# Value products behind the last projection in three loops, other banks in a fourth, and loads cut to a loop's rows, in a nested self-attention kernel

## The chip, the cores and the metric

The kernel runs on one core of a Trainium2 chip. The metric is device time in microseconds (us). Three runs of the kernel before took 325.38, 325.65 and 325.74 us, so the median is 325.65. One further execution was recorded by the hardware profiler: it took 326.82 us, of which 325.0 us are the recorded span. Every row of a trace that is quoted comes from that one execution.

Engine names in the rows: PE is TensorE (matmuls; PEld its weight loads), DVE is VectorE, ACT is ScalarE, POOL is GpSimd, SP is SyncE, which here only issues DMAs.

## The reference

32 sequences of up to 512 rows, 512 wide, 8 heads of 64. The lengths are drawn between 64 and 511, the same draw each time. Rows past a sequence's length stay zero.

```python
for b in range(batch):
    seq_len = lengths[b]
    x_b = x[b, :seq_len].copy()
    qkv = np.matmul(x_b, w_qkv)
    q, k, v = np.split(qkv, 3, axis=-1)
    ...
    scores = scale * np.matmul(q, k.transpose(0, 2, 1))
    scores_max = np.max(scores, axis=-1, keepdims=True)
    attn = np.exp(scores - scores_max)
    attn = attn / (np.sum(attn, axis=-1, keepdims=True) + 1e-08)
    out_b = np.matmul(attn, v).transpose(1, 0, 2).reshape(seq_len, dim)
    output[b, :seq_len] = out_b
```

## The kernel before

**Loops.** The sequences are sorted by length on the chip, longest first, and taken in 16 pairs, 0 to 15. There is one loop for each count of rows N in 512, 448, 384, 352, 320 and so on down to 96, and a pair runs in the smallest N that holds its longer sequence. In this draw pair 0 runs in 512, 1 in 448, 2 in 384, 3 to 5 in 352, 6 in 320, 7 in 288, 8 in 256, 9 and 10 in 224, 11 in 192, 12 and 13 in 160, 14 in 128 and 15 in 96. A sequence is held in tiles of 128 rows; a loop has one to four of them.

**Positions.** The body of a loop has two positions, one for each sequence of the pair. A position does the attention of its own sequence, and between these steps the projections of the next sequence, whose transposed `x` (`xT`) must have landed. Five sequences ahead, SP loads `x` (LD). GpSimd casts it to 16 bit under a mask (C, line 374), and SP issues the transposing DMAs (XT, line 331) that make `xT` for the position after next. XT waits for the position's last projection on TensorE, since that is the last reader of the buffer it writes, and for C.

**Order.** The order in a position is written out by hand, one string for each N in the table `ORDER`. A step is a letter, a number, and after `@` the PSUM banks (0 to 7) that it writes:

- `S`: scores (line 1280), then their exponentials on ScalarE (line 1298).
- `Q`, `K`, `V`: projections (lines 303 and 314); `B` (queries and keys together), `U`, `V0a`, `V0b` (values) the same in half rows, in parts a, b, c (line 1334); `W` the values of the shared last tile (line 1221). The results are cast out of the bank by ScalarE (a, or `*`) or by VectorE (d).
- `A`: value products (line 1528, in halves line 1642). Loops whose last tile holds 64 rows or fewer pack the last tiles of both sequences into one; `Z` (line 1568) adds that shared tile's part to the products of two `A` steps. Behind a completed `A`, or behind `Z` for both of its `A` steps, VectorE normalises: U (lines 1743, 1704), R (lines 1739, 1695) and O (line 1677, which writes `out_nat`). Only then may another step use the bank.
- `X`: issue XT. `D`: issue LD. `L`, `P`: masks on VectorE and C. `E`: some columns. At the end of a position SP issues the store ST (line 1125), which waits for the last O.

Each engine runs its steps in this order, in its own queue. A wait is put where a step needs what another engine makes, or a bank that another engine still reads; it is a semaphore compared with a count kept in a register. These registers are raised once a pair, at the loop's end. For TensorE `LATE` says how many of its last steps come behind the raising (lines 2155 and 2158).

**Loads.** `load` (line 1106) brings whole tiles, with one DMA. In the last pairs of a count of tiles, the shorter form with one tile less is taken. Semaphores are raised by 16 for a landed DMA.

The step that the argument comes back to most is `rest` (the `Z` step), in its core:

```python
def rest(h0):
    pavs = [sums[h0][1], sums[h0 + 2][1]]
    ...
    op(f"z{h0}", "PE", matmuls, tuple(reads), held)
    for h in (h0, h0 + 2):
        normed(h)
```

Of the kernel before, what the change touches and what calls it, by code (L numbers as in the profile page):

```python
# [18 lines left out]
P = 128  # L19
# [18 lines left out]
    passed: object = None  # L38


LATE = {288: 3, 224: 3, 192: 1, 160: 3}


def plan_waits(head, bodies, entries, rare):
# [136 lines left out]
def kernel(  # L181
# [8 lines left out]
    nc = tc.nc  # L190
    B, MAXS, D = x.shape
    NT = MAXS // P
# [14 lines left out]
    def ring(n, shape, dtype, name, pool=const):  # L207
        return [pool.tile(shape, dtype, name=f"{name}{k}") for k in range(n)]
# [5 lines left out]
    x_bufs = ring(2, [P, NT, D], FP32, "x_nat")  # L214
# [20 lines left out]
    xv = x.rearrange("b (t p) d -> b p t d", p=P)  # L235
# [46 lines left out]
    }  # L282
# [9 lines left out]
    def tiles(N):  # L292
        return -(-N // P)
# [28 lines left out]

    def unit(name):

        return 16 * NT if name[:2] == "XT" else 16 if name[:2] in ("LD", "ST", "ZT") else 1

    def transpose(name, xT, x16, n, rows=P, pairs_on=0):

# [56 lines left out]
    def before_loops():  # L385
# [4 lines left out]
        def op(name, eng, emit, reads=(), writes=(), dma=False):  # L390
            ops.append(Op(name, eng, emit, tuple(reads), tuple(writes), dma))
# [16 lines left out]
        sp, act, dve, pool = nc.sync, nc.scalar, nc.vector, nc.gpsimd  # L408
# [44 lines left out]
        def warm(name, source, count, repeats, after):  # L453
# [4 lines left out]
            def matmuls():  # L458
# [11 lines left out]
                out=t,  # L470
                in_=blank,
# [34 lines left out]
        def key(lens, ids):  # L506
# [20 lines left out]
                out=t, in0=key_row, scalar1=key_col, scalar2=None, op0=ALU.is_lt  # L527
# [60 lines left out]
        for n in range(NT, 0, -1):  # L588
            N = min(N for N in LOOPS if tiles(N) == n)
# [37 lines left out]
        found = {}  # L627
# [11 lines left out]
            op(name, "SP", load, ("order",))  # L639

        def fetch(name, b, at, k, t0, t1):
            op(
                name,
                "SP",
                lambda: sp.dma_start(
                    out=x_bufs[b][:, t0:t1, :],
                    in_=xv[bass.ds(found[at][k], 1), :, t0:t1, :].rearrange("o p t d -> (o p) t d"),
                ),
                (),
                [f"xn{b}", *(f"xn{b}.{t}" for t in range(t0, t1))]  # L650
                if t1 - t0 == NT
                else [f"xn{b}.{t}" for t in range(t0, t1)],
                dma=True,
            )
# [9 lines left out]
        for t in range(NT):  # L664
            fetch(f"x0.{t}", 0, 0, 0, t, t + 1)
# [3 lines left out]
        weights("wk", w_k, D, NC // 2, NC)  # L669
        numbers("n1", 1, 4)  # L670
        fetch("x1.0", 1, 1, 0, 0, NT // 2)
        fetch("x1.2", 1, 1, 0, NT // 2, NT)

        warm("warm1", ones16, 12, 1, ())
# [6 lines left out]
                out=t,  # L681
# [27 lines left out]
                out=t, in_=shifted.rearrange("p (g k) -> p g k", k=4), axis=AX.X, op=ALU.add  # L709
# [120 lines left out]
        def joined(name, low, high, bits, after, out=None):  # L830

            t = const.tile([P, B // 2], FP32, name=f"h_{name}") if out is None else out
            op(
                name,
                "DVE",
                lambda: dve.scalar_tensor_tensor(
                    out=t, in0=high, scalar=float(2**bits), in1=low, op0=ALU.mult, op1=ALU.add
                ),
                after,
                (name if out is None else "table",),  # L840
            )
            return t

        def twos(source):
            return [source.rearrange("p (j two) -> p j two", two=2)[:, :, k] for k in range(2)]
# [4 lines left out]
        later = joined("later", *twos(order_i[:, 6 : B + 6]), 5, ("order",))  # L850
# [28 lines left out]
                out=alive[:, 0:B, :],  # L879
# [11 lines left out]
                out=queries[:, 1, :], in0=alive[:, 0, :], scalar1=2.0, scalar2=-1.0, op0=ALU.mult, op1=ALU.add  # L891
# [8 lines left out]
                out=t,  # L900
                in_=more[:, (448 - (NT - 1) * P) // 32 % 4 :: 4, :].rearrange("p k j -> p j k"),
# [11 lines left out]
                out=m_bufs[0], in0=alive[:, 2, :], scalar1=0.0, scalar2=None, op0=ALU.add  # L913
# [8 lines left out]
                out=v_bufs[0][:, :, :, HD],  # L922
# [8 lines left out]
        for half in range(2):  # L931
            for own in range(2):
                at_ = 1 - (half ^ own)
                k = B // 2 - at_
                rows = slice(half * P // 2, (half + 1) * P // 2)
# [6 lines left out]
                        out=to,  # L942
# [95 lines left out]
    def position(N, j, at, ring):  # L1038
# [4 lines left out]
        n = tiles(N)  # L1043
# [7 lines left out]
        o = 1 - j  # L1051
# [43 lines left out]
        def unless_past(ahead, name, transfer):  # L1095

            with nc.If_lt(own_pair, (B - ahead - j + 1) // 2):
                last = transfer()
                if last is not None:
                    last.then_inc(sems[name], 16)  # L1100
            with nc.Else():
                nc.sync.sem_inc(sems[name], unit(name))
            nc.end_ifs()

        def load(k=n):
            return nc.sync.dma_start(
                out=x_bufs[o][:, 0:k, :],
                in_=xv[bass.ds(here["later"][j], 1), :, 0:k, :].rearrange("o p t d -> (o p) t d"),
            )

        def load_live():
            name = f"LD{j}"
            with nc.sync.If_cmp(of(here["pairs"], "SP"), here["until"], "IS_LT"):
                load().then_inc(sems[name], 16)
            with nc.sync.Else():
                load(n - 1).then_inc(sems[name], 16)
            nc.sync.end_ifs()
# [650 lines left out]
        def maybe(name, ahead, transfer):  # L1768
            return transfer if n > 1 else lambda: unless_past(ahead, name, transfer)
# [6 lines left out]
        for step in steps(N, j):  # L1776
            step = step.split("@")[0]
            kind, act = step[0], step.endswith("*")
            if step[2:3] in ("a", "b", "c"):
                name, engines = step[:2], step[4:]  # L1780
# [66 lines left out]
            elif kind == "X":  # L1847
                transfer = maybe(f"XT{j}", 3, transposed)
# [60 lines left out]
    here = {}  # L1909
# [13 lines left out]
    for v in range(len(LOOPS)):  # L1923
        later = {op.name for body in bodies[v:] for op in body[0] + body[1]}
# [7 lines left out]
    rare = {"Y0", "Y1", "w", "W0", "W1"}  # L1932
# [32 lines left out]
    sems = {name: tc.alloc_semaphore(f"done_{name}") for name in lead}  # L1965
# [6 lines left out]
    def value_of(v, j, wait):  # L1972

        name = wait[1]
        if name in rare and wait[0] in ("iter", "iterin"):
            return wait[0].replace("iter", "rare"), lead[name] + 1 - wait[2]
        if wait[0] == "pos":
            return "pos", lead[name] + 1 - wait[2] + j
        if wait[0] == "iter":
            return f"iter{unit(name)}", unit(name) * (lead[name] + 1 - wait[2])  # L1980
        if wait[0] in ("posin", "posold"):
            return wait[0], lead[name] + 1 - wait[2]
        if wait[0] == "iterin":
            return f"iterin{unit(name)}", unit(name) * (lead[name] + 1 - wait[2])
        if wait[0] == "lead":
            return None, lead[name] * unit(name)
        if wait[0] == "last":
            last = max(u for u in range(len(LOOPS)) if name in has[u])
            return f"end{last}", lead[name]
        return None, 1  # L1990


    raised = {"pos": 2, "rare": 1, "iter16": 16, f"iter{16 * NT}": 16 * NT}
    entered = {"posold": 0, "posin": 2, "rarein": 1, "iterin16": 16, f"iterin{16 * NT}": 16 * NT}

    tails_of = []
    for v, N in enumerate(LOOPS):
        mine = [k for k, op in enumerate(bodies[v][1]) if op.eng == "PE"]
        tails_of.append(mine[len(mine) - LATE.get(N, 0) :])
        assert not any(bodies[v][1][k].skip for k in tails_of[v])  # L2000
# [99 lines left out]
    with tc.tile_critical():  # L2100
# [59 lines left out]
        for v, N in enumerate(LOOPS):  # L2160
# [17 lines left out]
            with nc.body(body):  # L2178
# [4 lines left out]
                p = nc.snap(pair, min_val=0, max_val=B // 2 - 1)  # L2183
# [59 lines left out]
```

## Time and profile before

| | before |
|---|---|
| median of three runs | 325.65 us |
| the profiled execution, its own time | 326.82 us |
| its span | 325.0 us |
| mean granted TensorE clock | 0.993 |
| LD issues of 768 KB / 512 KB / 1024 KB | 12 / 14 / 3 |
| XT issues (line 331) | 74, about 1.25 us of SP each |

A row of the timeline gives the start (us from the span's start), the length in us (of all the merged instructions), the engine, the line, the operation with what it writes and reads, the shape, the count, and in brackets the idle time before it with what ended it. A row of the chain gives start, length, engine and what ran. Line numbers are those of the kernel before. Matmuls are pipelined, so a row's length reaches past the start of the next one; what a matmul group takes is read from start to start.

### The profile page before, as it was taken

The page shows a single profiled execution, that of the slowest core. Times are in us where ns is not written, and L with a number is a line of the kernel's source. Part 1 is how long each engine was busy: PE and PEld are TensorE (multiplying, and loading weights), DVE is VectorE, ACT ScalarE, POOL GpSimd, SP SyncE. Part 2 cuts the span into 40 slices and gives each one's busy share as a digit, 9 for nine tenths or more (in the row PEclk, how much of TensorE's full clock was granted, in tenths as well). Part 3 has the DMA queues.
Part 4 walks back from the last instruction along what each step waited for, and adds up shares of the span by engine and source line. Part 5 has one row for each costly group of instructions (what it writes and reads, how often), then busy time and mean ns, then how long its engine had stood idle before and what let it go on. Part 6 is the DMA issues. An engine that isn't in the chain of part 4 may idle for free.

```text
span 325.0 us, 13310 instructions
## 1 busy us (share of the span) xinstructions
PE 311.3 (96%) x5092; PEld 202.2 (62%) x5092; DVE 193.4 (60%) x650; ACT 264.0 (81%) x415; POOL 100.6 (31%) x147
## 2 busy tenths in 40 slices
PE   7999999999999999999999999999999899999991
PEld 4444645555656556556556657657787787877861
DVE  6866566566665546456456456436575666666753
ACT  4489899797878988988988979898877678777761
POOL 2657040414030330330330342143222223533420
PEclk9999999999999999999999999999999999999997
DMA  6986858497848999597677777756459957896652
GB/s 216 373 316 72 259 180 277 94 351 171 281 50 281 224 294 261 185 285 226 227 225 226 244 210 198 221 169 219 135 150 206 233 179 178 180 239 161 216 180 81
DMA packets 69448, 68.85 MB, mean 212 GB/s; under 512 B 40720, under 2 KB 40720, under 8 KB 69392
## 3 DMA queue, kind: packets, MB, share of 16 engines
q1 hardware_dynamic: 69344, 68.12, 74.8%
q8 instruction: 33, 0.54, 0.7%
q14 instruction: 23, 0.19, 0.2%
q10 hardware_dynamic: 48, 0.00, 0.0%
HBM read 25.17 MB, written 33.55 MB: 181 GB/s over the span
## 4 chain that ended last, share of the span: by engine, by line
PE 88%; DMA 4%; DVE 2%; issue 1%; ACT 1%; SPq 1%; POOL 0%; POOLq 0%; DVEq 0%
PE banks L1334 43%; PE banks L1280 14%; PE banks L1528 12%; PE banks L314 7%; PE banks L303 6%; DMA xT<-x 3%; PE banks L1642 3%; PE banks L1221 1%; PE banks L1568 1%; DMA x_nat<-in_x_dram 1%; DVE out_nat L1677 0%; PE banks L768 0%; ACT et L1298 0%; SPq L331 0%; ACT xT L777 0%
## 5 line engine op out<-in xcount | busy, mean ns | idle before, releaser
L1298 ACT ACTIVATE et<-banks 128x704 f16<-128x704 f32 (+8 forms) x256 | 199.1, 825 | 25.8 <-PE banks L1280 22.0
L374 POOL TENSOR_TENSOR x<-x_nat,mask 128x512 f16<-128x512 f32 x82 | 83.1, 1039 | 177.1 <-DVE mask L1062 170.0
L1334 PE MATMUL banks<-xT,w_r 64*128 64x352 f16 (+9 forms) x1536 | 127.7, 294 | 1.4 <-DMA xT<-x 1.0
L1334 PEld LDWEIGHTS banks<-xT,w_r 64*128 64x128 f16 x1536 | 68.9, 94 | 37.8 <-PE banks L1334 8.7
L1280 PE MATMUL banks<-qz,kT 64*128 64x352 f16 (+11 forms) x624 | 77.4, 294 | 1.3 <-ACT et L1298 0.4
L1677 DVE SCALAR_TENSOR_TENSOR out_nat<-rcp,banks 128x256 f32<-128x256 f32 (+1 forms) x128 | 59.4, 470 | 6.5 <-DMA out_dram<-out_nat 2.2
L1378 DVE CAST qz<-banks 128x448 f16<-128x448 f32 (+6 forms) x47 | 26.4, 562 | 46.6 <-PE banks L1334 45.8
L1528 PEld LDWEIGHTS banks<-v_aug,et 128*128 128x128 f16 x1248 | 42.0, 97 | 14.4 <-issue 7.2
L1528 PE MATMUL banks<-v_aug,et 128*128 128x65 f16 x1248 | 47.6, 194 | 0.7 <-ACT et L1298 0.6
L1334 PE MATMUL banks<-w_r,xT 64*128 64x512 f16 (+1 forms) x368 | 46.6, 372 | 0.3 <-ACT v_aug L1500 0.3
L1280 PEld LDWEIGHTS banks<-qz,kT 64*128 64x128 f16 x624 | 28.0, 94 | 24.0 <-issue 5.9
L1743 DVE TENSOR_TENSOR rcp<-banks,queries 128x4 f32<-128x4 f32 (+1 forms) x110 | 17.3, 157 | 19.8 <-PE banks L1528 7.3
L1397 DVE CAST v_aug<-banks 128x512 f16<-128x512 f32 x25 | 16.6, 690 | 19.2 <-PE banks L1334 19.2
L314 PE MATMUL banks<-w_r,xT 128*128 128x512 f16 x104 | 26.7, 380 | 0.0
L1334 PEld LDWEIGHTS banks<-w_r,xT 64*128 64x128 f16 x368 | 17.1, 94 | 14.5 <-PE banks L1334 1.0
L303 PE MATMUL banks<-xT,w_r 128*128 128x160 f16 (+3 forms) x256 | 23.2, 243 | 1.1 <-issue 0.6
L1378 ACT CAST kT<-banks 128x352 f16<-128x352 f32 (+6 forms) x47 | 22.5, 479 | 1.5 <-PE banks L1334 1.5
L1739 DVE RECIPROCAL rcp<-rcp 128x4 f32<-128x4 f32 (+1 forms) x110 | 20.2, 184 | 3.8
L1378 DVE CAST kT<-banks 128x352 f16<-128x352 f32 (+5 forms) x33 | 17.9, 552 | 7.7 <-PE banks L1334 7.6
L303 PEld LDWEIGHTS banks<-xT,w_r 128*128 128x128 f16 x256 | 16.5, 98 | 6.2 <-issue 1.2
L1378 ACT CAST qz<-banks 128x352 f16<-128x352 f32 (+6 forms) x33 | 15.3, 464 | 3.4 <-PE banks L1334 3.3
L1500 ACT CAST v_aug<-banks 128x512 f16<-128x512 f32 x15 | 8.9, 590 | 9.5 <-PE banks L314 9.5
(117 smaller groups left out, 180.4 us busy)
## 6 DMA issues: line engine op xcount, KB each, us to landing
x_nat<-in_x_dram SPq DMA_DIRECT2D x12, 768.0 KB, 6.7
out_dram<-out_nat SPq DMA_DIRECT2D x12, 768.0 KB, 4.1
x_nat<-in_x_dram SPq DMA_DIRECT2D x14, 512.0 KB, 4.6
out_dram<-zeros SPq DMA_DIRECT2D x12, 512.0 KB, 3.7
out_dram<-out_nat SPq DMA_DIRECT2D x12, 512.0 KB, 5.1
out_dram<-out_nat SPq DMA_DIRECT2D x4, 1024.0 KB, 6.8
x_nat<-in_x_dram SPq DMA_DIRECT2D x3, 1024.0 KB, 7.0
out_dram<-zeros SPq DMA_DIRECT2D x4, 768.0 KB, 4.5
```

Of the source, the lines that this page charges most:

```text
L303: last = nc.tensor.matmul(dst[:, 0:N], w_r[:, c, w0 : w0 + P], xT[:, c, 0:N], start=(c == 0), stop=(c == NC - 1),)
L314: last = nc.tensor.matmul(pv, xT[:, c, t * P : (t + 1) * P], w_r[:, c, 2 * D : 3 * D], start=(c == 0), stop=(c == NC - 1),)
L374: return engine.tensor_tensor(out=x16, in0=x32, in1=live.broadcast_to([P, D]), op=ALU.mult)
L1280: last = nc.tensor.matmul(psc[par][:, x * wide : x * wide + N], kT[r, i, c0 : c0 + P], qz[r, i, 0:N], start=True, stop=True,)
L1298: return nc.scalar.activation(out=et[:, :, x0:x1, 0:N], in_=got.rearrange("p j (x q) -> p j x q", q=wide)[:, :, x0:x1, 0:N], func=AF.Exp, ...
L1334: last = nc.tensor.matmul(to, lhs(rows, c), rhs(rows, c), start=(c == 0 and opens), stop=(c == NC - 1 and not opens),)
L1378: return lambda copy, bank: copy(out=buf[:, ms, 0:M], in_=bank[:, 0 : gm * M].rearrange("p (m q) -> p m q", q=M),)
L1397: return lambda copy, bank: copy(out=v_bufs[o][:, t, :, 0:HD], in_=bank.rearrange("p (h d) -> p h d", d=HD))
L1528: last = nc.tensor.matmul(pav[:, g, qt, :], e_bufs[e][:, c0 + qt * P : c0 + (qt + 1) * P], v_aug[:, kt, h, :], start=(kt == 0 and not (hal ...
L1677: return nc.vector.scalar_tensor_tensor(out=o_t[:, 0:n, h0 * HD : (h0 + heads) * HD].rearrange("p t (g d) -> p t g d", d=HD), in0=by, scal ...
L1739: return nc.vector.reciprocal(out=r, in_=total if n == 1 else r)
L1743: return nc.vector.tensor_tensor(out=r.rearrange("p (t g) -> p t g", t=n), in0=total.rearrange("p (t g) -> p t g", t=n), in1=rows, op=ALU. ...
```

## The change

Three kinds of edit are made together.

**The order.** In 256 (second position) the last half B1b goes ahead of A0b, and A4 and A6 go behind the last projection and behind the issue of XT and LD. In 192 (second position) V0a and V0b go ahead of A1a and A1b by one step each, so that A1b ends up behind XT and LD. In 160, A2 and Z0 go behind the last projection and XT in both positions. In 288 (first position) S3 is put in banks 6 and 7 in place of 5 and 6. `LATE` gets an entry for 256.

```diff
-LATE = {288: 3, 224: 3, 192: 1, 160: 3}
+LATE = {288: 3, 256: 2, 224: 3, 192: 1, 160: 3}
...
-        288: "L P D S0@56 B2a@24 S5@01 B2b:aa S3@56 B0a@01 S1@23 S9@45 B0b:dd S2@67 B1a@32 S6@45 B1b:da S4@67 "
+        288: "L P D S0@56 B2a@24 S5@01 B2b:aa S3@67 B0a@01 S1@23 S9@45 B0b:dd S2@67 B1a@32 S6@45 B1b:da S4@67 "
...
-        "A1b | L P S0@01 U0a@25 S1@34 U0b:ad B0a@76 S2@01 E0@4 B0b A0a@23 B0c:da B1a@45 S3@01 A0b B1b A4@6 "
-        "A6@7 B1c:aa X D",
+        "A1b | L P S0@01 U0a@25 S1@34 U0b:ad B0a@76 S2@01 E0@4 B0b A0a@23 B0c:da B1a@45 S3@01 B1b A0b B1c:aa "
+        "X D A4@6 A6@7",
...
-        "P B0a@50 S1@34 B0b S2@67 B0c:da W0@4 S0@12 B1a@03 S3@67 E0@5 B1b A0a@12 B1c:aa A0b A1a@46 V0a@57 A1b "
-        "V0b:aa X D",
-        160: "L P S0@01 S1@23 V0@5 Q0*@4 A0@0 K0*@7 A2@1 S2@23 Z0 K2*@6 Q2*@7 X D A4@5 A6@2 Z4 | L P S0@34 S1@67 "
-        "K2@0 Q2*@1 A0@3 W0*@4 Q0@6 A2@5 K0*@0 Z0 S2@12 V0*@6 X D A4@4 A6@7 Z4",
+        "P B0a@50 S1@34 B0b S2@67 B0c:da W0@4 S0@12 B1a@03 S3@67 E0@5 B1b A0a@12 B1c:aa A0b V0a@57 A1a@46 "
+        "V0b:aa X D A1b",
+        160: "L P S0@01 S1@23 V0@5 Q0*@4 A0@0 K0*@7 S2@23 K2*@6 Q2*@7 X D A2@1 Z0 A4@5 A6@2 Z4 | L P S0@34 S1@67 "
+        "K2@0 Q2*@1 A0@3 W0*@4 Q0@6 K0*@0 S2@12 V0*@6 X D A2@5 Z0 A4@4 A6@7 Z4",
```

**The loads.** Where N is no multiple of 128, the last tile is loaded by a DMA of its own, and only to row N. The semaphore of a load then counts to 32, and a load of one DMA adds 16 by an instruction of SP.

```diff
-        return 16 * NT if name[:2] == "XT" else 16 if name[:2] in ("LD", "ST", "ZT") else 1
+        units = {"XT": 16 * NT, "LD": 32, "ST": 16, "ZT": 16}
+        return units.get(name[:2], 1)
...
         def load(k=n):
+            name, rows = f"LD{j}", N - (n - 1) * P
+            batch = bass.ds(here["later"][j], 1)
+            if k < n or rows == P:
+                nc.sync.sem_inc(sems[name], 16)
+                return nc.sync.dma_start(
...
+                )
+            partial = nc.sync.dma_start(
+                out=x_bufs[o][0:rows, n - 1, :],
+                in_=xv[batch, 0:rows, n - 1, :].rearrange("o p d -> (o p) d"),
+            )
...
+            partial.then_inc(sems[name], 16)
             return nc.sync.dma_start(
-                out=x_bufs[o][:, 0:k, :],
-                in_=xv[bass.ds(here["later"][j], 1), :, 0:k, :].rearrange("o p t d -> (o p) t d"),
+                out=x_bufs[o][:, 0 : n - 1, :],
+                in_=xv[batch, :, 0 : n - 1, :].rearrange("o p t d -> (o p) t d"),
             )
```

What stands in the engines' queues: first TensorE at the end of 256's second position and into the 224 loop, before and then after the change. The 1642 (1666) rows are halves of A0b, shown as their last two; the 1334 (1358) rows are projections; 1528 (1552) are A4 and A6; the branch ends the loop.

```order
827 L1642 MATMUL banks<-v_aug_68,et_82 128x65
828 L1334 MATMUL banks<-xT_75,w_r 128x224 x16
829 L1528 MATMUL banks<-v_aug_68,et_83 128x65 x8
830 L1528 MATMUL banks<-v_aug_68,et_84 128x65 x8
831 L1334 MATMUL banks<-xT_75,w_r 128x224 x8
832 L2086 UNCONDITIONAL_BRANCH
```

```order
827 L1666 MATMUL banks<-v_aug_68,et_81 128x65
828 L1666 MATMUL banks<-v_aug_68,et_82 128x65
829 L1358 MATMUL banks<-xT_75,w_r 128x224 x8
830 L2179 ISA
831 L2182 REGISTER_ALU
832 L1552 MATMUL banks<-v_aug_68,et_83 128x65 x8
833 L1552 MATMUL banks<-v_aug_68,et_84 128x65 x8
834 L2110 UNCONDITIONAL_BRANCH
```

The last eight projections now stand ahead of the sixteen products of A4 and A6, and the raising of the registers ahead of those.

Then TensorE in 160's second position, from Q0 on, before and after. The `128x160` rows of line 303 are Q0 and K0, 1568 (1592) are Z0 and Z4, 314 is V0, and 1280 (1304) is S2.

```order
1103 L303 MATMUL banks<-xT_75,w_r 128x160 x8
1104 L1528 MATMUL banks<-v_aug_68,et_82 128x65 x4
1105 L303 MATMUL banks<-xT_75,w_r 128x160 x8
1106 L1568 MATMUL banks<-v_aug_67,et_82 128x65 x8
1107 L1280 MATMUL banks<-qz_66,kT_70 128x160 x4
1108 L314 MATMUL banks<-w_r,xT_75 128x512 x4
1109 L2155 ISA
1110 L2158 ISA
1111 L1528 MATMUL banks<-v_aug_68,et_82 128x65 x8
1112 L1568 MATMUL banks<-v_aug_67,et_82 128x65 x8
```

```order
1103 L303 MATMUL banks<-xT_75,w_r 128x160 x16
1104 L1304 MATMUL banks<-qz_66,kT_70 128x160 x4
1105 L314 MATMUL banks<-w_r,xT_75 128x512 x4
1106 L1552 MATMUL banks<-v_aug_68,et_82 128x65 x4
1107 L1592 MATMUL banks<-v_aug_67,et_82 128x65 x8
1108 L2179 ISA
1109 L2182 ISA
1110 L1552 MATMUL banks<-v_aug_68,et_82 128x65 x8
1111 L1592 MATMUL banks<-v_aug_67,et_82 128x65 x8
```

A2 (four products) and Z0 (eight) went from between the projections to behind V0, the last of them. The queues of VectorE, ScalarE and GpSimd are the same as before.

More of the change, by code (lines that the diff above doesn't have):

```diff
@@ L641, in fetch, with transfer @@
         def fetch(name, b, at, k, t0, t1):
+            def transfer():
+                if name in sems:
+                    sp.sem_inc(sems[name], 16)
+                return sp.dma_start(
+                    out=x_bufs[b][:, t0:t1, :],
+                    in_=xv[bass.ds(found[at][k], 1), :, t0:t1, :].rearrange("o p t d -> (o p) t d"),
+                )
             op(
@@ L644, in fetch @@
                 "SP",
[L645 to L648, printed above, removed]
+                transfer,
                 (),
@@ L1105, in load @@
         def load(k=n):
+            name, rows = f"LD{j}", N - (n - 1) * P
[3 more added lines that the diff above has]
+                return nc.sync.dma_start(
+                    out=x_bufs[o][:, 0:k, :],
+                    in_=xv[batch, :, 0:k, :].rearrange("o p t d -> (o p) t d"),
+                )
+            partial = nc.sync.dma_start(
+                out=x_bufs[o][0:rows, n - 1, :],
+                in_=xv[batch, 0:rows, n - 1, :].rearrange("o p d -> (o p) d"),
+            )
+            if n == 1:
+                nc.sync.sem_inc(sems[name], 16)
+                return partial
+            partial.then_inc(sems[name], 16)
             return nc.sync.dma_start(
-                out=x_bufs[o][:, 0:k, :],
-                in_=xv[bass.ds(here["later"][j], 1), :, 0:k, :].rearrange("o p t d -> (o p) t d"),
+                out=x_bufs[o][:, 0 : n - 1, :],
+                in_=xv[batch, :, 0 : n - 1, :].rearrange("o p t d -> (o p) t d"),
             )
@@ L1990, in value_of @@
         return None, 1
-    raised = {"pos": 2, "rare": 1, "iter16": 16, f"iter{16 * NT}": 16 * NT}
-    entered = {"posold": 0, "posin": 2, "rarein": 1, "iterin16": 16, f"iterin{16 * NT}": 16 * NT}
+    raised = {"pos": 2, "rare": 1, "iter16": 16, "iter32": 32, f"iter{16 * NT}": 16 * NT}
+    entered = {"posold": 0, "posin": 2, "rarein": 1, "iterin16": 16, "iterin32": 32, f"iterin{16 * NT}": 16 * NT}
     tails_of = []
```

## The prediction

> **What bounds the kernel now.** I read the page first (busy shares, then the chain that ended last), then the waits, then the timelines at the five places where the order changes.
>
> ```profile
> PE 311.3 (96%) x5092; PEld 202.2 (62%) x5092; DVE 193.4 (60%) x650; ACT 264.0 (81%) x415; POOL 100.6 (31%) x147
> ...
> PE   7999999999999999999999999999999899999991
> ...
> PE 88%; DMA 4%; DVE 2%; issue 1%; ACT 1%; SPq 1%; POOL 0%; POOLq 0%; DVEq 0%
> ```
>
> TensorE is busy for 311.3 of 325.0 us and holds 88% of the chain. The change takes no matmul away, so it can only shorten what is left, 13.7 us. Of the 40 slices of 8.1 us the first is 0.7 busy and the last 0.1, so most of that is the start and the end. Of the transposing DMA (line 331), which the change issues earlier, the view of that line says who waits:
>
> ```profile
>   PE banks L1334: 1.0, 1
>   PE banks L303: 0.5, 1
> DMA to landing us min/median/max: 2.3/3.1/7.3
> ```
>
> TensorE waits for it twice, for 1.0 and 0.5 us. The other side of the ledger is VectorE: a value product that runs later is normalised later, and the bank that it filled comes free later. So each edit is weighed by two things: what an earlier transpose pays, and what a later normalisation costs.
>
> **256, second position (before the 224 loop).** Timeline of TensorE, then the chain, then SP:
>
> ```profile
> 243.89 0.66 PE L1528 MATMUL banks<-v_aug,et 128*128 128x65 f16 x16
> 244.48 1.05 PE L1334 MATMUL banks<-xT,w_r 64*128 64x224 f16 x16
> ...
> 250.74 1.13 PE L1642 MATMUL banks<-v_aug,et 64*128 64x65 f16 x64
> 252.82 0.56 PE L1334 MATMUL banks<-xT,w_r 64*128 64x224 f16 x8 [0.96 <-DMA xT<-x]
> ```
> ```profile
> 245.18 1.21 SPq L331
> 246.43 6.25 DMA xT<-x
> ```
> ```profile
> 241.56 0.42 SPq L1106 DMA_DIRECT2D x_nat<-in_x_dram  x1
> 242.23 0.38 SPq L1125 DMA_DIRECT2D out_dram<-out_nat  x1
> ```
>
> A4 and A6 (16 matmuls, 243.89 to 244.48, so 0.59 us) move behind the last projection, so SP may issue the transposes 0.59 sooner. The wait at 252.82 is 0.96, so all 0.59 could come out of it. But this transpose lands 6.25 us after its issue, against a median of 3.1, behind a load (241.56) and a store (242.23) of 512 KB each. What the queue still holds doesn't leave earlier because the transposes come earlier. The gain is therefore between 0 and 0.59; I take **-0.2**, the lower third, because the load and the store stand ahead either way.
>
> The Trainium skill, "DMA: Bandwidth & Descriptors", section "Two DMAs through the same engine are not ordered", says that within one queue of one DMA engine descriptors start in order. By that alone the term would be 0, and by an idle queue 0.59; the 6.25 us of this row side with the page.
>
> The same edit swaps A0b with B1b (16 projections, 0.77 in the chain). Its normalisation starts 0.77 later:
>
> ```profile
> 243.68 0.75 DVE L1677 SCALAR_TENSOR_TENSOR out_nat<-rcp,banks 128x256 f32<-128x256 f32 x2
> 247.74 0.62 DVE L1378 CAST qz<-banks 128x448 f16<-128x448 f32 x1 [0.43 <-PE banks L1334]
> ```
>
> It ends at 244.43 now and at 245.2 then, and the 224 loop's first projection (near 244.97, bank 3) needs that bank: up to 0.27 lost, and VectorE's cast at 247.74 slips by up to 0.7. Both lie ahead of the wait of 0.96, which absorbs them. If that cover is gone, they cost 0.3. The counters raised two operations ahead only move two register instructions off the loop's end: at most 0.1, counted at nothing.
>
> **288, other banks.** S3 goes to banks 6 and 7, so S9 no longer waits for S3's exponential:
>
> ```profile
> 212.99 0.30 PE L1280 MATMUL banks<-qz,kT 64*128 64x288 f16 x2 [0.36 <-ACT et L1298]
> ```
> ```profile
> 212.25 2.95 ACT L1298 ACTIVATE et<-banks 128x576 f16<-128x576 f32 x5
> 215.46 1.74 ACT L1298 ACTIVATE et<-banks 128x576 f16<-128x576 f32 x3
> ```
>
> The 0.36 goes, but ScalarE runs its exponentials back to back there (five in 2.95 us), so TensorE meets the next one instead. Between 0 and 0.36; I take **-0.05**.
>
> **192, second position.** V0b moves ahead of A1b:
>
> ```profile
> 284.20 0.31 PE L1642 MATMUL banks<-v_aug,et 64*128 64x65 f16 x8
> 284.46 0.61 PE L1334 MATMUL banks<-w_r,xT 64*128 64x256 f16 x8
> ...
> 290.06 0.37 PE L303 MATMUL banks<-xT,w_r 128*128 128x160 f16 x3 [0.65 <-issue]
> ```
>
> The projection, and the transpose that waits for it, come 0.26 sooner (284.46 less 284.20). No TensorE wait stands behind this transpose, and 0.65 us of waiting for nothing that the profile shows stands soon after, which can swallow it. Between 0 and 0.26; I take **-0.05**.
>
> **160, both positions: the largest term.** A2 and Z0 go behind the last projection. Z0 completes the shared last tile, and the whole normalisation chain (L1743, L1739, L1677, four times, 0.74 us each) starts only after it. TensorE of pairs 12 and 13 and of the 128 loop, then VectorE:
>
> ```profile
> 291.26 1.28 PE L303 MATMUL banks<-xT,w_r 128*128 128x160 f16 x16
> ...
> 294.70 0.30 PE L1568 MATMUL banks<-v_aug,et 64*128 64x65 f16 x8
> ...
> 295.07 1.04 PE L314 MATMUL banks<-w_r,xT 128*128 128x512 f16 x4
> 295.94 0.41 PE L1528 MATMUL banks<-v_aug,et 128*128 128x65 f16 x8
> ...
> 297.09 1.04 PE L314 MATMUL banks<-w_r,xT 128*128 128x512 f16 x4
> ...
> 309.54 1.03 PE L314 MATMUL banks<-w_r,xT 128*128 128x512 f16 x4
> ...
> 311.63 1.53 PE L303 MATMUL banks<-xT,w_r 128*128 128x96 f16 x32 [0.48 <-DMA xT<-x]
> ```
> ```profile
> 289.97 0.42 DVE L1677 SCALAR_TENSOR_TENSOR out_nat<-rcp,banks 128x256 f32<-128x256 f32 x1 [1.14 <-DMA out_dram<-out_nat]
> ...
> 295.04 0.16 DVE L1743 TENSOR_TENSOR rcp<-banks,queries 128x4 f32<-128x4 f32 x1 [0.42 <-PE banks L1568]
> ...
> 295.87 0.42 DVE L1677 SCALAR_TENSOR_TENSOR out_nat<-rcp,banks 128x256 f32<-128x256 f32 x1 [0.46 <-DMA out_dram<-out_nat]
> ...
> 296.61 0.42 DVE L1677 SCALAR_TENSOR_TENSOR out_nat<-rcp,banks 128x256 f32<-128x256 f32 x1
> ...
> 308.40 0.42 DVE L1677 SCALAR_TENSOR_TENSOR out_nat<-rcp,banks 128x256 f32<-128x256 f32 x1
> ```
>
> End of pair 12. Without A2 (0.12) and Z0 (0.13 to the next start) ahead of it, the projection at 295.07 starts at 294.82 and runs 0.87 (to the next start, 295.94); A2 starts at 295.69, Z0 at 295.81, and 0.34 later, as now, VectorE: 296.15 in place of 295.04. The first normalisation comes 0.41 behind that (295.87 less 295.04 less the wait of 0.46, rounded up), at 296.56; it no longer waits for the store, so of the 1.11 only 0.69 is late. The second starts at 297.30 and ends at 297.72. The next position's first projection (V0, bank 5) needs that second one. It starts at 297.09, just behind the 297.03 where it ends now: there is no slack. So **+0.7** (0.5 to 0.9, by how early TensorE really reaches Z0).
>
> Inside pair 12 Z0 goes from before the 16 projections (to 290.26) to behind them, so the normalisation at 289.97, now held 1.14 by a store, would start near 290.8, and the second end near 291.95; the second half of the projections at 291.26 (eight, from about 291.8) needs it: 0.1. VectorE's later key cast, which the projection just before Z0 waits for, gives another 0.1. Pair 13 is alike: together **+0.4** (0.1 to 0.6).
>
> Before the 128 loop the last normalisation ends at 308.82; moved like the first by 1.11 it ends at 309.9, and V0 at 309.54 waits for it: +0.4. In exchange the wait of 0.48 for the transpose at 311.63 goes, since its issue is 0.25 sooner and TensorE comes 0.4 later: **-0.1** (-0.48 to +0.3, the latter if the next transpose slips as well).
>
> **Loads.** Six in 352, four in 224 and two in 192 become two DMAs and bring 64 to 128 KB less.
>
> ```profile
> x_nat<-in_x_dram SPq DMA_DIRECT2D x12, 768.0 KB, 6.7
> x_nat<-in_x_dram SPq DMA_DIRECT2D x14, 512.0 KB, 4.6
> ```
> ```profile
> POOL x L374 <- DMA x_nat<-in_x_dram: 7.1, 2, 4.8
> ```
>
> The loads are issued five sequences ahead and land in 4.6 to 6.7 us; the only two waits for one, on GpSimd, are in the start, whose loads are not cut. What remains is SP's time, one issue more (0.4, as at 241.56) ahead of the next transposes, against some fewer bytes: bounds -0.2 and +0.4, taken as **0**.
>
> **The sum**: -0.2 - 0.05 - 0.05 + 0.7 + 0.4 - 0.1 + 0 = **+0.7**. The profiled execution took 326.82 us (span 325.0), so it would be 327.5 under a profile; the median of the runs is 325.65, so 326.35. 0.2% of this kernel is 0.65 us, about what a measurement can tell from no change: the forecast lies just above that bound.
>
> **Rivals.**
>
> *B, the transposes pay and the lag is covered: faster.* In full, the gains are 0.59 (256), 0.36 (288), 0.26 (192) and 0.48 (128 loop's wait), together 1.69. If Z0's lag finds cover (the normalisation, freed of the store's 0.46, is late by less than 0.3, which decides it), some 0.4 of stalls remain: -1.3, 324.35. For it: two real transpose waits. Against it: V0 at 297.09 has 0.06 of slack.
>
> *C, nothing to measure.* Half of the gain (0.8) meets half of the loss (0.6 to 0.8), or the wait of 0.65 at 290.06 shrinks by as much as the new ones cost: 325.65, give or take 0.3.
>
> *D, SP becomes late too: slower.*
>
> ```profile
> 287.99 1.18 SPq L1106 DMA_DIRECT2D x_nat<-in_x_dram  x1
> ...
> 291.58 3.97 SPq L331 DMA_TRANSPOSE xT<-x  x2
> ```
> ```profile
> DMA to landing us min/median/max: 2.3/3.5/4.7
> ```
>
> These transposes (291.58, and the second at 294.36, landed 2.3 later at 296.7) feed V0 at 297.09. The load at 287.99 held SP for 1.18; cut in two, it may hold it that long twice, and the transposes then land near 297.9, behind even the late normalisation (297.72). It decides from 1.1 us of delay. Here it costs 0.2 more than A, and the other ten cut loads at 0.05 to 0.1 each bring the sum to +1.4 to +1.9: 327.3. Against it: other loads are issued in 0.4.
>
> The Trainium skill, "SBUF — State Buffer", section "Summary: rules for kernel authors", speaks against cutting a transfer: "one DMA, not several". By the fit in that page's section "The DMA setup-cost knee", 2 us and the bytes over 436 GB/s, I estimate 3.2 us for 512 KB and 2.4 and 2.6 us for the two parts; the trace shows 4.6 for the whole, and nobody waiting for it.
>
> **Chances.** Forecast A 0.55 (from +0.1 to +1.2; 0.22 of it within 0.2%), B 0.2, C 0.15, D 0.1. So faster 0.2, same 0.22 + 0.15 = 0.37, slower 0.33 + 0.1 = 0.43. For 8 in 10 the range cuts half of B and most of D: 324.6 to 327.1.
>
> **What would show it.** Right: V0 at the start of pair 13 waits about 0.7 for `out_nat`, V0 of the 128 loop for the same, the wait of 0.48 there is gone, and the 0.96 before 252.82 is shorter by 0.2 (0.59 would be the gain in full, 0 the queue's). S9 in 288 has no wait, and a later score has one. Wrong: no wait for `out_nat` at pair 13, which gives B, or transposes issued later than now with the landing waited for, which gives D.

## The result

The changed kernel is slower: 328.61 us (median of 14 runs, 327.21 to 331.46) against 325.89 (14 runs of the kernel before). The ratio is 1.0076, with a 95% interval of 1.0054 to 1.0099, so +2.5 us (1.8 to 3.2; the two medians alone differ by 2.7). The direction was the one forecast; the size, +0.7, was far too small, and the time lies outside the range. The profiled execution took 328.77 us, its span 326.7.

The page of the changed kernel, for the rows shown of before:

```profile
PE 312.3 (96%) x5092; PEld 201.7 (62%) x5092; DVE 194.5 (60%) x650; ACT 263.7 (81%) x415; POOL 100.8 (31%) x147
...
PE   7999999999999999999999999999999999899982
...
PE 88%; DVE 5%; issue 2%; ACT 2%; DMA 1%; POOL 0%; SPq 0%; DVEq 0%; POOLq 0%
```

With the same matmuls TensorE is busy 1.0 us longer, and in the chain VectorE went from 2% to 5% while the DMAs went from 4% to 1%. In these two executions waits for the transpose went, and waits for VectorE came. (Lines moved: 1280 is now 1304, 1334 is 1358, 1528 is 1552, 1568 is 1592, 1677 is 1701, 1739 is 1763, 1500 is 1524; 303 and 314 stayed.)

**Where it came from.** The view by stretches, cut at three starts that both kernels have: the first scores of pair 12's second position, of pair 13, and of the 128 loop, up to the first projections for 96. The columns are the length and the busy time of TensorE, its weight loads, VectorE, ScalarE and GpSimd (counts in brackets), the granted clock, the DMA share and GB/s. Before:

```profile
290.74:296.49 5.75, 5.75 (x101) 4.71 (x98) 3.82 (x18) 4.32 (x8) 2.44 (x3) 1.00 0.76 185
296.49:307.42 10.93, 10.73 (x184) 8.73 (x178) 8.26 (x36) 8.80 (x15) 4.97 (x6) 1.00 0.64 196
307.42:311.63 4.21, 3.74 (x60) 2.93 (x61) 2.72 (x11) 2.60 (x5) 1.04 (x1) 1.00 0.84 255
```

After:

```profile
290.60:296.76 6.16, 6.15 (x100) 4.75 (x96) 3.96 (x18) 4.36 (x7) 2.45 (x4) 1.00 0.60 181
296.76:308.73 11.97, 11.51 (x184) 8.76 (x179) 7.74 (x34) 8.39 (x14) 4.97 (x6) 1.00 0.68 218
308.73:313.50 4.77, 3.91 (x64) 2.96 (x61) 3.79 (x16) 2.59 (x5) 1.04 (x1) 1.00 0.61 177
```

The same work takes 20.89 us before and 22.90 after: +0.41, +1.04 and +0.56, at a clock of 1.00 in both. Between these two executions the span grew by 1.7 us (325.0 to 326.7), so the 2.0 us of these stretches are more than all of it, and the rest of the span came out 0.3 shorter. Four kinds of row make them up. First, TensorE at the start of pair 13, as forecast:

```profile
295.80 0.28 PE L1552 MATMUL banks<-v_aug,et 128*128 128x65 f16 x4
296.01 0.30 PE L1592 MATMUL banks<-v_aug,et 64*128 64x65 f16 x8
296.24 0.42 PE L1552 MATMUL banks<-v_aug,et 128*128 128x65 f16 x8
296.60 0.30 PE L1592 MATMUL banks<-v_aug,et 64*128 64x65 f16 x8
296.76 0.86 PE L1304 MATMUL banks<-qz,kT 64*128 64x160 f16 x12
297.98 1.04 PE L314 MATMUL banks<-w_r,xT 128*128 128x512 f16 x4 [0.36 <-DVE out_nat L1701]
```

From the scores to V0 it was 0.60 (296.49 to 297.09) and is 1.22: V0 waits 0.36 idle, and the scores, whose second half needs the bank of the first normalisation, take 0.86, of which 0.3 are a wait for `out_nat`.

Second, in the same rows, a cost that the forecast did not have: A2's four products take 0.21 to the next start (295.80 to 296.01), where they took 0.12 in the forecast's reading, and Z0 takes 0.23, not 0.13. Z0 (64 rows) now stands between two groups of 128 rows; before, it stood next to S2, which also has 64.

Third, inside the pair, the projections behind the second position's scores:

```profile
291.11 1.47 PE L303 MATMUL banks<-xT,w_r 128*128 128x160 f16 x16
292.41 0.29 PE L1552 MATMUL banks<-v_aug,et 128*128 128x65 f16 x4
```

They take 1.30 to the next start, where they took 1.12 (291.26 to 292.38). About 0.2 of that is a wait for `out_nat`, between the first eight and the last eight.

Fourth, the 128 loop:

```profile
311.43 1.02 PE L314 MATMUL banks<-w_r,xT 128*128 128x512 f16 x4 [0.40 <-DVE out_nat L1701]
...
313.50 1.53 PE L303 MATMUL banks<-xT,w_r 128*128 128x96 f16 x32 [0.46 <-DVE v_aug L1524]
```

V0 waits 0.40 for the last normalisation, as forecast. But the wait of 0.48 for the transpose did not go: one of 0.46 for VectorE stands in its place. A wait of 0.20 for ScalarE ahead of that loop's first scores (307.42 before) is gone, since TensorE comes later.

Ahead of the 224 loop TensorE has two new waits, for the normalisation and for VectorE's cast, and the wait of 0.96 for the transpose is gone:

```profile
245.03 0.56 PE L1358 MATMUL banks<-xT,w_r 64*128 64x224 f16 x8 [0.32 <-DVE out_nat L1701]
...
248.96 1.04 PE L1358 MATMUL banks<-w_r,xT 64*128 64x512 f16 x8 [0.45 <-DVE qz L1402]
```

### The profile page after: what moved, and what is told of

Its sections match the earlier page's. It is cut to its first block, busy times and chain, and to the rows that moved or that the text cites. A ratio compares the mean times of both kernels' runs of the same rounds, so it can differ in the third digit from the quotient of the medians.

```text
span 326.7 us, 13366 instructions
## 1 busy us (share of the span) xinstructions
PE 312.3 (96%) x5092; PEld 201.7 (62%) x5092; DVE 194.5 (60%) x650; ACT 263.7 (81%) x415; POOL 100.8 (31%) x147
## 4 chain that ended last, share of the span: by engine, by line
PE 88%; DVE 5%; issue 2%; ACT 2%; DMA 1%; POOL 0%; SPq 0%; DVEq 0%; POOLq 0%
PE banks L1358 43%; PE banks L1304 13%; PE banks L1552 12%; PE banks L314 7%; PE banks L303 5%; PE banks L1666 3%; DVE out_nat L1701 2%; PE banks L1245 1%; PE banks L1592 1%; DMA x_nat<-in_x_dram 1%; DVE rcp L1763 1%; ACT et L1322 1%; PE banks L774 0%; DVE v_aug L1524 0%; ACT x L374 0%
```

## The experiments

Each kernel was timed in five rounds against the kernel before. A difference in us is worked out from the ratio, so it can be some tenths away from the difference of two medians. The theories: late normalisation in 160 carries the loss; or the cut loads do; or the other loops.

### The parts alone

The edit of 160 alone:

```diff
-        160: "L P S0@01 S1@23 V0@5 Q0*@4 A0@0 K0*@7 A2@1 S2@23 Z0 K2*@6 Q2*@7 X D A4@5 A6@2 Z4 | L P S0@34 S1@67 "
-        "K2@0 Q2*@1 A0@3 W0*@4 Q0@6 A2@5 K0*@0 Z0 S2@12 V0*@6 X D A4@4 A6@7 Z4",
+        160: "L P S0@01 S1@23 V0@5 Q0*@4 A0@0 K0*@7 S2@23 K2*@6 Q2*@7 X D A2@1 Z0 A4@5 A6@2 Z4 | L P S0@34 S1@67 "
+        "K2@0 Q2*@1 A0@3 W0*@4 Q0@6 K0*@0 S2@12 V0*@6 X D A2@5 Z0 A4@4 A6@7 Z4",
```

> The kernel before with the edit of 160 alone. If the late normalisation in 160 carries the loss: +1.5 to +2.5 us (0.7 at pair 13's start, 0.4 inside the pairs, 0.5 at the 128 loop, and some 0.2 per position for a 64-row matmul group that now stands alone between 128-row groups). If the loads or the other loops carry it: under +0.7. In the trace by the first theory: V0 of pair 13 waits 0.3 to 0.4 for out_nat, V0 of the 128 loop 0.4.

328.22 us (six runs) against 326.21, ratio 1.0057 (1.0038 to 1.0076): +1.9 us. Its three stretches take 6.17, 11.95 and 4.79, so 22.91 us, the same as the whole change to 0.01, with nearly the same waits (0.36, 0.43 and 0.46).

The loads alone (only the loads' hunks of the diff):

```diff
+            partial = nc.sync.dma_start(
+                out=x_bufs[o][0:rows, n - 1, :],
...
+            partial.then_inc(sems[name], 16)
```

> The kernel before with the cut loads alone. If the loads only cost SP's time, hidden: within 0.3 us of before. If they disturb the queue or the supply of instructions: +0.7 to +1.5, with more spread between runs, and longer waits for nothing shown (issue) on TensorE in 224 and 192.

328.02 us, ratio 1.0047 (1.0025 to 1.0069): +1.5 us. The cut loads, taken as free, are not. TensorE has one long new wait, ahead of 96's projections, and it is for the transpose:

```profile
307.15 5.26 DMA xT<-x
312.42 0.26 issue
312.68 1.53 PE banks L303 x32
```
```profile
312.68 1.53 PE L303 MATMUL banks<-xT,w_r 128*128 128x96 f16 x32 [1.53 <-DMA xT<-x]
```

The first rows are from the chain (start, length, what ran), the last from TensorE's timeline. Ahead of 307.15 the chain runs through SP, not TensorE.

256's order and its entry in `LATE` alone:

```diff
-        "A1b | L P S0@01 U0a@25 S1@34 U0b:ad B0a@76 S2@01 E0@4 B0b A0a@23 B0c:da B1a@45 S3@01 A0b B1b A4@6 "
-        "A6@7 B1c:aa X D",
+        "A1b | L P S0@01 U0a@25 S1@34 U0b:ad B0a@76 S2@01 E0@4 B0b A0a@23 B0c:da B1a@45 S3@01 B1b A0b B1c:aa "
+        "X D A4@6 A6@7",
```

> The kernel before with 256's order and its entry in LATE alone. If the earlier transpose pays its wait of 0.96 less the new waits of 0.32 and 0.45: -0.2 to -0.4. If the lead is given back at the next stall of instruction supply, as in the profile of after (0.54 at 254.4): 0 to +0.2.

326.40 us, ratio 1.0017 (1.0001 to 1.0033): not a gain, rather +0.5. Both new waits are there (0.32 and 0.45), and no wait for the transpose. No wait for nothing shown (issue) followed in this profile, so that reading was not borne out. The interval reaches almost to no change, and the size of this cost is uncertain.

288's banks and 192's order alone:

```diff
-        288: "L P D S0@56 B2a@24 S5@01 B2b:aa S3@56 B0a@01 S1@23 S9@45 B0b:dd S2@67 B1a@32 S6@45 B1b:da S4@67 "
+        288: "L P D S0@56 B2a@24 S5@01 B2b:aa S3@67 B0a@01 S1@23 S9@45 B0b:dd S2@67 B1a@32 S6@45 B1b:da S4@67 "
...
-        "P B0a@50 S1@34 B0b S2@67 B0c:da W0@4 S0@12 B1a@03 S3@67 E0@5 B1b A0a@12 B1c:aa A0b A1a@46 V0a@57 A1b "
-        "V0b:aa X D",
+        "P B0a@50 S1@34 B0b S2@67 B0c:da W0@4 S0@12 B1a@03 S3@67 E0@5 B1b A0a@12 B1c:aa A0b V0a@57 A1a@46 "
+        "V0b:aa X D A1b",
```

> The kernel before with the edits of 288 and 192 alone. By the profile of after 288 gains 0.2. 192 by the forecast: 0 to -0.26; if it costs, as the later start of 160 in the profile of after suggests (0.4 more of a stall at 283): +0.2 to +0.4. So -0.4 to +0.2 in all.

325.70 us against 326.21, ratio 1.0002 (0.9979 to 1.0024): nothing to measure. The trace has a possible reason why a small lead made in 288 does not show: TensorE comes to pair 12's second position early and waits there for the transpose.

```profile
289.69 1.27 PE L303 MATMUL banks<-xT,w_r 128*128 128x160 f16 x16 [0.37 <-DMA xT<-x]
```

### Parts taken out of the whole

> The change without its edit of 160 (so the loads, 256, 288 and 192 remain). If 160 and the loads each cost by themselves and cover one another in part: between +0.8 and +1.8 us, like the loads alone. If the loss of the loads was only scatter: within 0.5 of before.

Without 160's edit: 326.94 us, ratio 1.0024 (1.0006 to 1.0043), +0.8. The loads remain, and so does their wait: 1.33 for the transpose ahead of 96's projections. But this kernel holds the loads and 256's edit, which cost +1.5 and +0.5 alone; +2.0 is outside the interval here (0.2 to 1.4). So these two don't add either, or one of them is smaller than it looked; no run decides which.

> The whole change but for the loads. If 160's late normalisation covers what the cut loads cost at the end: 0.2 to 0.4 us less than the whole change, so +1.8 to +2.3 against before. If the two add: 1.5 less, +1.0.

Without the loads: 328.58 us, ratio 1.0081 (1.0054 to 1.0107), as slow as the whole change (1.0076). Its stretches take 22.91 us. So the loads cost 1.5 alone and nothing that can be measured on top of 160: where the normalisation in 160 is late, TensorE reaches 96's projections after the transpose has landed. In the profile of the whole change it landed at 312.4 (issued 307.97, 4.4 to landing), and the projections start at 313.50. Both are delays into one meeting point, and the later one counts.

### What in 160 costs

S2 and Z0 taken apart, nothing moved behind the last projection:

```diff
-        160: "L P S0@01 S1@23 V0@5 Q0*@4 A0@0 K0*@7 A2@1 S2@23 Z0 K2*@6 Q2*@7 X D A4@5 A6@2 Z4 | L P S0@34 S1@67 "
-        "K2@0 Q2*@1 A0@3 W0*@4 Q0@6 A2@5 K0*@0 Z0 S2@12 V0*@6 X D A4@4 A6@7 Z4",
+        160: "L P S0@01 S1@23 V0@5 Q0*@4 A0@0 K0*@7 S2@23 A2@1 Z0 K2*@6 Q2*@7 X D A4@5 A6@2 Z4 | L P S0@34 S1@67 "
+        "K2@0 Q2*@1 A0@3 W0*@4 Q0@6 A2@5 S2@12 K0*@0 Z0 V0*@6 X D A4@4 A6@7 Z4",
```

> The kernel before, with the 64-row groups S2 and Z0 of 160 no longer next to each other, each between 128-row groups, while Z0 stays ahead of the last projections and its end moves by at most 0.25 us. If a change between 64-row and 128-row matmuls costs TensorE about 0.09 us by itself: TensorE's starts in pairs 12 and 13 stretch by 0.19 per position, +0.5 to +0.9 in all. If only the late normalisation costs: 0 to +0.3.

326.96 us, ratio 1.0029 (1.0005 to 1.0052): +0.9 (0.2 to 1.7). TensorE in pair 13's first position, then the same groups before:

```profile
298.95 0.72 PE L303 MATMUL banks<-xT,w_r 128*128 128x160 f16 x8
299.60 0.31 PE L1280 MATMUL banks<-qz,kT 64*128 64x160 f16 x4
299.84 0.30 PE L1528 MATMUL banks<-v_aug,et 128*128 128x65 f16 x4
300.07 0.30 PE L1568 MATMUL banks<-v_aug,et 64*128 64x65 f16 x8
300.30 1.28 PE L303 MATMUL banks<-xT,w_r 128*128 128x160 f16 x16
```
```profile
298.64 0.72 PE L303 MATMUL banks<-xT,w_r 128*128 128x160 f16 x8
299.19 0.29 PE L1528 MATMUL banks<-v_aug,et 128*128 128x65 f16 x4
299.41 0.31 PE L1280 MATMUL banks<-qz,kT 64*128 64x160 f16 x4
299.56 0.29 PE L1568 MATMUL banks<-v_aug,et 64*128 64x65 f16 x8
299.78 1.28 PE L303 MATMUL banks<-xT,w_r 128*128 128x160 f16 x16
```

The same four groups take 1.35 us (298.95 to 300.30) and 1.14 (298.64 to 299.78), with no wait in either: 0.21 more. Between 64-row and 128-row matmuls the order before changes twice there (into S2, out of Z0), this one four times, so an added change costs about 0.1. Whether TensorE has to empty at a change, or two groups of 64 rows side by side overlap, these rows can't tell. In the three stretches it is 21.37 us, +0.48: 0.21 in each of three positions, less 0.15 at the start of pair 13, where the way to V0 became that much shorter. So the changes of kind do cost, by themselves about a quarter of the 2.0. The rest is late normalisation by the rows above (V0 of pair 13 and of 128, the projections inside the pairs); no run has it without the changes of kind.

160's edit in the second position alone (its second line of the diff above):

> The kernel before with the edit of 160 in the second position alone. If the late normalisation at the end of a pair decides: V0 of pair 13 waits for out_nat (0.3 to 0.4 seen, 0.7 late in all) and V0 of 128 waits 0.4, so +1.0 to +1.7, most of what the whole edit of 160 costs (2.0). If it is the same for both positions: half, +1.0 or less, and the first position carries the rest.

327.27 us, ratio 1.0033 (1.0015 to 1.0051): +1.1 (0.5 to 1.7), which both readings allow; the trace says more. V0 of pair 13 waits 0.36 and V0 of 128 waits 0.42, as in the whole edit; the stretches take 5.91, 11.50 and 4.78, so 22.19, +1.30. Of the 2.0 us of the whole edit in these stretches the other 0.7 need the first position's edit too.

### What in the loads costs

192's two loads cut, the others whole:

```diff
-            if k < n or rows == P:
+            if k < n or rows == P or N != 192:
```

> The kernel before with the counts of the loads, but only 192's two loads cut in two. If the loss of the loads comes from SP's queue after 192 (transposes up to pair 14 issued 0.3 to 0.5 later, the one that TensorE waits for before 96's projections landing up to 1 us later): +0.7 to +1.7, as with all loads cut. If it comes from the ten cut loads in 352 and 224, or from the start: 0 to +0.4.

326.66 us, ratio 1.0013 (0.9986 to 1.0040): +0.4 (-0.5 to +1.3), by time alone inconclusive. Its trace has the wait, 1.23, for the transpose of 305.95, and the chain ahead of it is SP's own work:

```profile
304.34 0.37 SPq L1118
...
304.98 0.40 SPq L1149
...
305.95 5.20 DMA xT<-x
311.15 0.26 issue
```

It has a longer one too, 1.48 for a transpose in pair 12. But the kernel below that only counts differently, with all loads whole, has 1.25 there, so that wait is not put down to the cut loads:

```profile
290.29 1.27 PE L303 MATMUL banks<-xT,w_r 128*128 128x160 f16 x16 [1.48 <-DMA xT<-x]
```
```profile
290.71 1.27 PE L303 MATMUL banks<-xT,w_r 128*128 128x160 f16 x16 [1.25 <-DMA xT<-x]
```

The reverse, 352's and 224's ten loads cut and 192's whole:

```diff
-            if k < n or rows == P:
+            if k < n or rows == P or N == 192:
```

> The kernel before with the ten loads of 352 and 224 cut, 192's two whole. If only a cut load just ahead of 160 costs, where SP has no time to spare: -0.2 to +0.4 us, and no wait above 0.5 for the transpose ahead of 96's projections. If every cut load costs a share: about ten twelfths of the loss of the loads alone (1.5), +1.2.

326.10 us against 326.29, ratio 0.9991 (0.9955 to 1.0026): no cost that can be measured (-1.5 to +0.8). A share of ten twelfths, +1.2, is outside the interval. Its profile, of an execution that took 330.24 us, has no wait for the transpose ahead of 96's projections, as the first reading expected. Over all profiles of kernels that leave 160's moved groups where they were, the picture is the same: 1.53, 1.33 and 1.23 for that transpose in the three with 192's loads cut, and at most the 0.48 of before in the seven with them whole.

The count of 32 with whole loads:

```diff
-            if k < n or rows == P:
+            if True:
```

> The kernel before with the loads whole, but their semaphore counted to 32 and 16 of it added by an instruction of SP. If the 0.2 us more around the span, seen in every kernel with cut loads, come from the counting: +0.2, all of it around the span. If from the cut DMAs: 0, and 1.84 us around the span as before.

326.46 us, ratio 0.9994 (0.9963 to 1.0025), 1.80 us around the span: no cost of the counting can be measured, and the 0.2 around the span are not its.

### A version ahead of both?

288's banks, and 256 with A4 and A6 late but A0b and B1b not swapped:

```diff
-        "A1b | L P S0@01 U0a@25 S1@34 U0b:ad B0a@76 S2@01 E0@4 B0b A0a@23 B0c:da B1a@45 S3@01 A0b B1b A4@6 "
-        "A6@7 B1c:aa X D",
+        "A1b | L P S0@01 U0a@25 S1@34 U0b:ad B0a@76 S2@01 E0@4 B0b A0a@23 B0c:da B1a@45 S3@01 A0b B1b B1c:aa "
+        "X D A4@6 A6@7",
```

> The kernel before with 288's banks, and 256 with A4 and A6 behind the last projection but A0b and B1b left in their order, and its entry in LATE. If the swap of A0b and B1b made the waits of 0.32 and 0.45 in 224, both are gone: -0.2 (288) and up to -0.3 more from the earlier transpose, so -0.5 to -0.1, a version ahead of both kernels. If the late A4 and A6 made them: 0 to +0.5.

325.96 us against 326.29, ratio 0.9988 (0.9963 to 1.0013): ahead of the changed kernel, not shown to be ahead of the one before. Of the two waits in 224, only the one of 0.32 belongs to the swap:

```profile
249.11 1.04 PE L1334 MATMUL banks<-w_r,xT 64*128 64x512 f16 x8 [0.46 <-DVE qz L1378]
```

The one of 0.45 stays: A4 and A6, normalised last, hold VectorE up at the loop's end, and its first cast in 224 is late.

## Why the prediction was wrong

**160, start of pair 13: right.** +0.7 was forecast, +0.62 came, at V0 and by the chain that was named. **Inside the pairs** the +0.4 forecast was right as well: the projections after the second position's scores take 0.18 more in each pair, and those ahead of S2 0.06 more (VectorE's later key cast would explain it, but no row shows that wait), so about 0.5 in all.

**160, the step that failed first: the moved groups were priced at their old durations.** A2 and Z0 were taken as 0.12 and 0.13 us wherever they stand. Z0 beside S2 shared its changes between 64-row and 128-row matmuls; alone it has its own, about 0.2 more in each of four positions (0.21 with the groups apart, 0.19 in the rows of the changed kernel), so some 0.8 in all. The Trainium skill, "TensorEngine Tiling (Array Packing)", section "Key Properties", says that changing the tiling mode drains TensorE; the rows of the kernel with the groups apart fit that, and give the price. The forecast had no such term.

**128, the step that failed second: "in exchange the wait of 0.48 goes".** V0 came 0.58 later behind the loop's first scores (2.12 us before, 2.70 after), and the stretch from V0 to 96's projections stayed as it was (2.09 us before, 2.07 after). Behind the transpose stood another chain, V0 and then its cast on VectorE, 0.07 us shorter. VectorE's row, and the transpose in the chain of before:

```profile
310.61 0.69 DVE L1500 CAST v_aug<-banks 128x512 f16<-128x512 f32 x1 [0.91 <-PE banks L314]
```
```profile
306.86 4.51 DMA xT<-x
```

That cast ended at 311.30 and the transpose landed at 311.37. In six other kernels that leave 160's groups ahead of the last projections and 192's loads whole, the cast is the later one, and the wait is 0.46 without any delay; here the row of the kernel with only 288 and 192:

```profile
310.03 1.53 PE L303 MATMUL banks<-xT,w_r 128*128 128x96 f16 x32 [0.46 <-DVE v_aug L1500]
```

So the wait of 0.48 had hardly anything to give. Removing the later of two nearly equal waits gains their difference, and delaying the shorter chain costs in full. So the term is +0.56, not -0.1. Together: 0.41 and 1.04 and 0.56 in the three stretches, +2.0 (after the 0.20 for ScalarE that went), where the forecast had +1.0 for all of 160.

**256: a gain that was one execution's.** The forecast took 0.2 out of a wait of 0.96. In the profiles of kernels that leave 256 alone the same wait is 0.27 (only 160), 0.20 (only 288 and 192), 0.16 (second position of 160), and none is shown in the other five (the loads alone, 192's alone, those of 352 and 224, the count, the groups apart). The two costs that were seen, 0.27 and up to 0.7, were said to lie under that cover, and the cover was mostly not there: they came as 0.32 and 0.45, the second by the late A4 and A6 and not by the swap, and the edit alone costs rather 0.5. The weighing of the queue against the 0.59 fell too: the second transpose of that position landed at 252.7 before and about 250.5 after (issued 245.5, landed 5.0 later), 2 us sooner, where the issue was only 0.9 sooner. The slow landing was that execution's as well: 6.25 us against at most 5.6 for these transposes in the thirteen other profiles.

**288** went as reasoned (S9's wait gone, a new one of 0.19 at the moved S3) and gained 0.2 in the trace of the changed kernel, not 0.05. **192** was not run by itself; together with 288 nothing shows in the time.

**The loads: 0 was right inside this change, but by luck.** The reason given, one issue more on SP against fewer bytes, left out the wait that the loads alone bring. Rival D named the place (192's cut load holds SP up ahead of 160) but asked for 1.1 us of delay. A few tenths do: with the loads alone that transpose was issued at 307.15 in place of 306.86 and took 5.26 in place of 4.51. The longer landing is the larger part. It goes with SP being late: the store ahead of that transpose is issued 0.26 to 0.49 us behind the start of V0 in the three profiles with 192's loads cut and 160 as it was, 0.06 behind it in the profile of before, and 0.4 to 1.5 ahead of it in the six others with the loads whole. That the late store makes the landing late is argued from these rows, not shown. The chain ahead of the transpose is SP's own work, which leaves no gap to make a delay good, and the waiting lies at the 128 loop, not at pair 13. Only 160's own lateness hides it. The Trainium skill's "one DMA, not several" ("SBUF — State Buffer", section "Summary: rules for kernel authors"), which stands there for DMA-bound transfers, points the right way where SP has no gap, at 192's loads; at the ten others no cost could be measured.

By these runs: 160's edit +1.9, 256's +0.5, 288's and 192's 0, the loads 0 behind 160's: +2.4, against +2.5 measured. Each of these terms has an interval of half a us or more to either side, so that they agree to 0.1 is in part luck. Against the forecast's +0.7, the terms that failed are the price of the moved groups (nothing forecast, some 0.8 measured), 128 (-0.1 against +0.56) and 256 (-0.2 against +0.5).

## What to carry over

Moving a matmul group behind the last projection moves everything that hangs on its bank: follow the normalisation to the next user of each bank, and price the moved group by its new neighbours. A wait in one profiled execution is not yet a reserve: look at the second-latest condition of the same wait, and at the same row in other profiles, before counting it as a gain or as a cover. Where several engines meet with little slack, two delays don't add; take each out alone and both together.

## What the runs showed of the hardware beside this

- A change between 64-row and 128-row matmuls cost TensorE about 0.1 us in these rows, without any row that shows a wait; in the stretches of that kernel it counts as busy.
- Around the span lie 1.8 us in eleven of the kernels, and 2.03 to 2.07 in the three with all loads cut (the loads alone, the change without 160, the whole change). The kernels with only some loads cut, or only the count, have 1.80 to 1.81. Why is open; it is 0.2 of the 1.5 us of the loads alone.
- Waits for nothing shown come and go at the same matmul. Value products near 283 waited 0.31 so in the profile of before, 0.70 after, 0.86 with only 160, 0.59 with only the loads, 0.96 with the groups apart, 0.31 with 160's second position, and show no such wait in the eight others. No run isolates the cause.
